# Seven products in the second and third feed-forward layers, input sums made over four tiles, and the modulation stream moved into the down projections

## The chip, the cores and the metric

The kernel runs on one core of one Trainium2 chip. The metric is device time in microseconds (us), the median over several runs. The engines are named as the profile names them: PE (TensorE, matrix products), PEld (its weight loads), DVE (VectorE), ACT (ScalarE), POOL (GpSimd) and SP (SyncE, which here issues the DMA transfers). Each engine works through its own queue of instructions in order.

## The reference

Two encoder layers, each of a feed-forward network (FFN), a mixer and a second FFN, on x of 512 tokens by 1024 channels, float32. The mixer is a state-space layer (SSM) in the first layer, an attention in the second. The core of it:

```python
def modulate(x, m): return x * (1 + m[:, 1][:, None, :]) + m[:, 0][:, None, :]
def swiglu(u, w_gate, w_up, w_down):
    return (jax.nn.silu(u @ w_gate) * (u @ w_up)) @ w_down
cond = jax.nn.silu(c)
for i in range(DEPTH):                                   # DEPTH = 2
    mods = (cond @ ada_w[i] + ada_b[i]).reshape(b, N_SUB, 3, D_MODEL)
    gate = lambda s: (1 + mods[:, s, 2])[:, None, :]
    y = swiglu(modulate(x, mods[:, 0]), ffn_w_gate[i, 0], ffn_w_up[i, 0], ffn_w_down[i, 0])
    x = layer_norm(ALPHA * x + 0.5 * gate(0) * y, ln_g[i, 0], ln_b[i, 0])
    u = modulate(x, mods[:, 1])
    y = mamba2_bidir(...) if i % 2 == 0 else diff_attention(...)
    x = layer_norm(ALPHA * x + gate(1) * y, ln_g[i, 1], ln_b[i, 1])
    y = swiglu(modulate(x, mods[:, 2]), ffn_w_gate[i, 1], ffn_w_up[i, 1], ffn_w_down[i, 1])
    x = layer_norm(ALPHA * x + 0.5 * gate(2) * y, ln_g[i, 2], ln_b[i, 2])
```

The FFN's inner width is 2816 = 22 x 128. `mods` is the product of the vector `cond` with a 1024 x 9216 matrix in each layer.

## The kernel before

Activations lie transposed: 8 arrays of 128 channels by 512 tokens. A float32 product is made of three products in a shorter format: every operand is split into a high part (`hi`, `uh`, `wh`: a copy by ACT) and the rest (`lo`, `ul`, `wl`: a subtraction on DVE), and `mm3` (L162) multiplies hi by hi, hi by lo and lo by hi.

The six parts of the program are numbered n = 0 to 5: FFN, SSM, FFN, FFN, attention, FFN. Below they are FFN0, FFN2, FFN3 and FFN5. An FFN has 22 tiles (f0 to f21), each of 128 columns of the inner width, cut into three parts of 8, 7 and 7 tiles. A part makes its tiles (gate and up products, `h = silu(gate) * up` at L538, and the split of h) and then its share of the down projection: 8 units of 128 output channels, each added to the residual stream `resid` by `add_res` (L366). In the last part of each FFN the layer norm (`LN`) is worked in, half the tokens at a time.

There are two ways to make a tile:

- The standard tile: 48 products of 512 columns: 8 input blocks, 3 products each, for gate and for up. Its two weight arrays (`wgu`, 128 x 1024 each) are loaded to `raw`, and `split` makes `wh` on ACT (L119) and `wl` on DVE (L120).
- The tile of seven products (`seven`): with the input cut in halves of the inner dimension and of the tokens, the two-by-two block product is made of 7 products instead of 8, as in Strassen's method: 7 x 4 blocks x 3 = 84 products of 256 columns. It needs sums of the weights (`weight_forms`: four additions on DVE in place, L461, and four splits, L451 and L452) for each tile, sums of products (L484 to L500), and sums of the inputs once per FFN (`input_forms`, L427 to L432).

`input_forms` makes four sets, one for each pair of input blocks k and k + 4. A set is 2 additions of 128 x 512 (`ft`, `fb`), 4 additions or subtractions of 128 x 256, and two splits. Before the change only FFN5 uses the seven products, from tile f4 on (`first7=4`), and all four sets are written at its tile f1.

The adaLN modulation `mods` is a stream of 144 loads of 512 KB (`adaw`), each followed by one multiply-and-sum on DVE over 128 x 1024 (`ada_unit`, L180). `advance(stream, k)` takes the next k of them. 16 are made at the start; FFN0 takes 3 per tile, FFN2 and FFN3 take 2 per tile after tile f3; these 72 belong to the second layer.

All loads of weights and of the stream go through one ring of 4 buffers (`raw`), issued by SP in program order (L93); the split weights have 3 + 3 buffers; temporary arrays (`tmp`) 6. At the start of FFN2, FFN3 and FFN5, POOL rescales the residual stream, 16 instructions (L359, L360 in `residual`). The scheduler of the framework, not the program text alone, sets the order of the instructions in each engine's queue; waits between engines follow from the data.

## Time and profile before

| | |
|---|---|
| median of 3 runs | 2255.68 us (2252.91 to 2257.87) |
| the profiled execution's own time | 2252.16 us |
| its span, first to last instruction | 2250.4 us |
| mean granted TensorE clock | 0.992 of full speed |
| PE busy | 2190.8 us, 97% |
| DVE busy | 1477.0 us, 66% |
| ACT busy | 900.0 us, 40% |
| POOL busy | 408.1 us, 18% |
| DMA, mean | 132 GB/s |

A busy share is an average over stages with different limits; the stages are read one by one in the rows below. Idle time of an engine costs nothing unless others wait for what it does next. "Releaser" names what ended an engine's wait, by the profile.

### The profile page before, as it was taken

The page shows a single profiled execution, that of the slowest core. Times are in us where ns is not written, and L with a number is a line of the kernel's source. Part 1 is how long each engine was busy: PE and PEld are TensorE (multiplying, and loading weights), DVE is VectorE, ACT ScalarE, POOL GpSimd, SP SyncE. Part 2 cuts the span into 40 slices and gives each one's busy share as a digit, 9 for nine tenths or more (in the row PEclk, how much of TensorE's full clock was granted, in tenths as well). Part 3 has the DMA queues.
Part 4 walks back from the last instruction along what each step waited for, and adds up shares of the span by engine and source line. Part 5 has one row for each costly group of instructions (what it writes and reads, how often), then busy time and mean ns, then how long its engine had stood idle before and what let it go on. Part 6 is the DMA issues. An engine that isn't in the chain of part 4 may idle for free.

```text
span 2250.4 us, 30448 instructions
## 1 busy us (share of the span) xinstructions
PE 2190.8 (97%) x11734; PEld 1825.4 (81%) x11734; DVE 1477.0 (66%) x2358; ACT 900.0 (40%) x1480; POOL 408.1 (18%) x412
## 2 busy tenths in 40 slices
PE   7999999999999989999999999999999999899998
PEld 5788888866777778888889888888877779889897
DVE  6865557656675788354558544545866679959696
ACT  4422223567656543222233222223555544525353
POOL 2000003344322336000015200003300025000003
PEclk9999999999999999999999999999999999999999
DMA  8865552465544416354642545542211121323231
GB/s 300 284 207 168 188 189 77 113 183 141 161 122 130 127 57 216 123 178 130 196 122 84 188 151 160 157 132 84 67 57 57 57 64 50 113 85 106 92 114 46
DMA packets 88529, 296.75 MB, mean 132 GB/s; under 512 B 9536, under 2 KB 12992, under 8 KB 88384
## 3 DMA queue, kind: packets, MB, share of 16 engines
q1 hardware_dynamic: 88384, 294.81, 42.2%
q8 instruction: 92, 1.51, 0.3%
q14 instruction: 53, 0.43, 0.1%
HBM read 289.53 MB, written 5.24 MB: 131 GB/s over the span
## 4 chain that ended last, share of the span: by engine, by line
PE 68%; DVE 7%; issue 4%; POOL 2%; ACT 1%; DMA 0%; POOLq 0%; ACTq 0%; DVEq 0%
PE acc L162 58%; PE mid L162 3%; PE mid L781 1%; DVE ul L350 1%; DVE wl L120 1%; PE mid L930 1%; PE ln L162 1%; DVE lt L348 1%; PE ln L249 1%; POOL E L770 1%; PE ln L729 1%; DVE lo L150 0%; DVE sc L292 0%; DVE resid L321 0%; ACT wh L119 0%
## 5 line engine op out<-in xcount | busy, mean ns | idle before, releaser
L119 ACT ACTIVATE wh<-raw 128x1024 fp32r<-128x1024 f32 (+1 forms) x306 | 316.0, 1035 | 752.9 <-PE acc L162 479.7
L162 PE MATMUL acc<-uh,wl 128*128 128x512 f32 (+1 forms) x1544 | 583.9, 378 | 7.4 <-DVE wl L120 7.4
L162 PE MATMUL acc<-uh,wh 128*128 128x512 f32 (+1 forms) x1544 | 587.3, 381 | 0.0
L162 PE MATMUL acc<-ul,wh 128*128 128x512 f32 (+1 forms) x1544 | 585.0, 379 | 0.4 <-DVE ul L1038 0.4
L120 DVE TENSOR_TENSOR wl<-raw,wh 128x1024 fp32r<-128x1024 f32 (+1 forms) x306 | 374.1, 1224 | 151.7 <-ACT wh L119 140.1
L162 PE MATMUL acc<-hi,wh 128*128 128x512 f32 (+1 forms) x1200 | 424.1, 354 | 6.1 <-DVE resid L366 6.1
L162 PE MATMUL acc<-hi,wl 128*128 128x512 f32 (+1 forms) x1200 | 423.7, 353 | 0.0
L162 PE MATMUL acc<-lo,wh 128*128 128x512 f32 (+1 forms) x1200 | 423.2, 353 | 0.0
L162 PEld LDWEIGHTS acc<-uh,wl 128*128 128x128 f32 x1544 | 291.8, 189 | 66.2 <-DVE wl L120 8.7
L162 PEld LDWEIGHTS acc<-uh,wh 128*128 128x128 f32 x1544 | 291.6, 189 | 63.4 <-issue 9.4
L162 PEld LDWEIGHTS acc<-ul,wh 128*128 128x128 f32 x1544 | 292.1, 189 | 58.4 <-issue 4.7
L180 DVE SCALAR_TENSOR_TENSOR raw<-raw,cond 128x1024 f32<-128x1024 f32 x144 | 178.1, 1241 | 160.9 <-DMA raw<-in_adaw 160.3
L162 PEld LDWEIGHTS acc<-hi,wh 128*128 128x128 f32 x1200 | 228.6, 191 | 40.6 <-DVE resid L366 6.5
L162 PEld LDWEIGHTS acc<-hi,wl 128*128 128x128 f32 x1200 | 229.0, 191 | 31.0 <-issue 1.2
L162 PEld LDWEIGHTS acc<-lo,wh 128*128 128x128 f32 x1200 | 228.9, 191 | 31.0 <-issue 0.8
L366 DVE SCALAR_TENSOR_TENSOR resid<-acc,gv,resid 128x512 f32<-128x512 f32 (+1 forms) x172 | 113.4, 661 | 123.9 <-PE acc L162 123.4
L112 POOL TENSOR_TENSOR wal<-raw,wah 128x512 fp32r<-128x512 f32 x13 | 21.4, 1649 | 879.1 <-ACT wah L110 879.1
L538 DVE TENSOR_TENSOR h<-sg,acc 128x512 f32<-128x512 f32 x65 | 44.5, 686 | 115.1 <-PE acc L162 114.8
L451 ACT ACTIVATE wh<-raw 128x1024 fp32r<-128x1024 f32 x54 | 57.1, 1059 | 85.5 <-PE acc L162 58.1
L162 PE MATMUL acc<-uh,wah 128*128 128x256 f32 (+1 forms) x232 | 65.4, 304 | 13.4 <-ACT wah L110 11.5
L277 POOL TENSOR_TENSOR resid<-resid,m 128x512 f32<-128x512 f32 x12 | 20.6, 1737 | 293.6 <-ACT m L274 292.0
L359 POOL TENSOR_TENSOR resid<-resid,rs 128x512 f32<-128x512 f32 x40 | 65.3, 1653 | 39.0 <-ACT rs L353 39.0
(270 smaller groups left out, 3189.3 us busy)
## 6 DMA issues: line engine op xcount, KB each, us to landing
raw<-in_wgu SPq DMA_DIRECT2D x176, 512.0 KB, 4.2
raw<-in_adaw SPq DMA_DIRECT2D x144, 512.0 KB, 4.4
raw<-in_wdn SPq DMA_DIRECT2D x64, 448.0 KB, 3.4
raw<-in_win SPq DMA_DIRECT2D x40, 512.0 KB, 4.0
raw<-in_wdn SPq DMA_DIRECT2D x32, 512.0 KB, 4.4
rw<-scr SPq DMA_DIRECT2D x32, 512.0 KB, 5.6
ch<-scr SPq DMA_DIRECT2D x32, 256.0 KB, 3.6
raw<-in_wso SPq DMA_DIRECT2D x16, 512.0 KB, 3.7
```

The costliest lines, as they stand in the source:

```text
L119: nc.scalar.activation(hi[:, :n], raw, AF.Copy)
L120: nc.vector.tensor_tensor(out=lo[:, :n], in0=raw, in1=hi[:, :n].bitcast(F32), op=ALU.subtract)
L162: last = nc.tensor.matmul(o, lhsT=a, rhs=b, start=start and j == 0, stop=j == n - 1, skip_group_check=not start)
L180: nc.vector.scalar_tensor_tensor(out=raw, in0=raw, scalar=1.0, in1=cond, op0=ALU.mult, op1=ALU.mult, accum_out=mods[l][:, j : j + 1],)
L249: nc.tensor.matmul(o[:, j * P : (j + 1) * P], lhsT=cols[:, j : j + 1].broadcast_to([P, P]), rhs=ident, start=True, stop=True)
L348: nc.vector.scalar_tensor_tensor(out=t, in0=res[d][:, a:b], scalar=G, in1=rb, op0=ALU.mult, op1=ALU.mult)
L350: nc.vector.scalar_tensor_tensor(out=ul, in0=t, scalar=B, in1=uh.bitcast(F32), op0=ALU.add, op1=ALU.subtract)
L359: nc.gpsimd.tensor_tensor(out=res[d], in0=res[d], in1=self.rs, op=ALU.mult)
L366: nc.vector.scalar_tensor_tensor(out=res[d][:, a:b], in0=pd[:, a:b], scalar=gvec[n][:, d : d + 1], in1=res[d][:, a:b], op0=ALU.mult, op1=A ...
L451: nc.scalar.activation(x[0], r, AF.Copy)
L538: nc.vector.tensor_tensor(out=h, in0=sg, in1=pu, op=ALU.mult)
L729: nc.tensor.matmul(pst, lhsT=bt[:, i * P : (i + 1) * P], rhs=xd, start=o == 0, stop=o == 1)
```

## The change

It calls FFN2 and FFN3 with `first7=4` too, so their tiles f4 to f21 become tiles of seven products. The four sets of input sums are no longer written at tile f1, but one at a time behind `h` of the four tiles before `first7`: f0 to f3 in FFN2, FFN3 and FFN5. The condition no longer asks whether the FFN has tiles of seven products at all. FFN0 keeps the default `first7=22`, and so writes four sets at its tiles f18 to f21 that nothing reads. The stream takes two numbers: per standard tile, and per down unit of the first two parts. FFN0 stays at 3 per tile. FFN2 and FFN3 take 1 per standard tile (4 of them) and 2 per down unit (16 units), 36 each, and none in their tiles of seven.

```diff
     def input_forms(u):
-        forms = []
         for k in range(4):
             top, bot = tmp("ft"), tmp("fb")
...
-            forms.append({
+            yield {
                 1: half(u[k], 0), 2: half(u[k + 4], 0), 3: half(u[k + 4], 1),
                 5: half((th, tl), 0), 7: half((th, tl), 1), 4: half((bh, bl), 0), 6: half((bh, bl), 1),
-            })
-        return forms
+            }
...
-    def ffn(n, stream=None, per=0, pre=None, first7=FT):
+    def ffn(n, stream=None, per=(0, 0), pre=None, first7=FT):
+        forms, making = [], None
...
             for _ in range(nf):
-                if f == 1 and first7 < FT:
-                    forms = input_forms(u)
                 if f >= first7:
...
                     f += 1
-                    advance(stream, per)
                     continue
...
                 hs.append(split_act(h))
+                if first7 - 4 <= f < first7:
+                    making = making or input_forms(u)
+                    forms.append(next(making))
                 f += 1
-                if f > 3:
-                    advance(stream, per)
+                if f > 3 or n > 0:
+                    advance(stream, per[0])
...
             for _ in down_units(n, hs, [mk(d) for d in range(KT)], pi == len(FPARTS) - 1):
-                pass
+                if pi < 2:
+                    advance(stream, per[1])
...
-    ffn(0, st0, 3, [[k[j] for k in ks] for j in range(8)])
+    ffn(0, st0, (3, 0), [[k[j] for k in ks] for j in range(8)])
...
-    ffn(2, st1, 2)
-    ffn(3, st1, 2)
+    ffn(2, st1, (1, 2), first7=4)
+    ffn(3, st1, (1, 2), first7=4)
```

How it moves instructions is seen in the queues' order. On DVE in FFN2, before the change, the stretch from tile f3's `h` holds splits of weights (L120), splits of `h` (L150) and products of the stream (L180):

```order
L538 TENSOR_TENSOR h_7649<-sg_7647,acc_7622 128x512
L120 TENSOR_TENSOR wl_7822<-raw_7819,wh_7821 128x1024
L150 TENSOR_TENSOR lo_7652<-h_7649,hi_7651 128x512
L180 SCALAR_TENSOR_TENSOR raw_7959,mods1_87<-raw_7959,cond_73 128x1024
L180 SCALAR_TENSOR_TENSOR raw_7962,mods1_87<-raw_7962,cond_73 128x1024
L120 TENSOR_TENSOR wl_7892<-raw_7889,wh_7891 128x1024
```

After the change, around tile f2's and f3's `h` (L535 now), the same queue holds the third set of input sums (L426 to L431), and the weight sums (L459) and splits (L450) of the first tile of seven, f4, whose raw weights are `raw_7795` and `raw_7797`; `wl_7908` and `w4l_7914` are the next tile's:

```order
L429 TENSOR_TENSOR ft_7687<-ft_7687,fb_7688 128x256
L459 TENSOR_TENSOR raw_7797<-raw_7797,raw_7795 128x512
L430 TENSOR_TENSOR fb_7688<-fb_7688,ft_7687 128x256
L150 TENSOR_TENSOR lo_7696<-ft_7687,hi_7695 128x512
L431 TENSOR_TENSOR fb_7688<-fb_7688 128x256
L459 TENSOR_TENSOR raw_7795<-raw_7797,raw_7795 128x512
L450 TENSOR_TENSOR wl_7802<-raw_7797,wh_7801 128x1024
L150 TENSOR_TENSOR lo_7700<-fb_7688,hi_7699 128x512
L459 TENSOR_TENSOR raw_7795<-raw_7795 128x512
L450 TENSOR_TENSOR wl_7908<-raw_7903,wh_7907 128x1024
L450 TENSOR_TENSOR w4l_7914<-raw_7905,w4h_7913 128x512
L450 TENSOR_TENSOR wl_7804<-raw_7795,wh_7803 128x1024
```

The last row, `wl_7804`, is the third weight form of f4, and the set's sums and another tile's splits now stand ahead of it. On PE after the change, the first product of f4 (into `acc_7819`) needs only the direct weights; the second (into `acc_7820`) starts at the 13th product of f4 and needs the third form, `wh_7803` and `wl_7804`:

```order
L162 MATMUL acc_7819<-uh_7160,wh_7799 128x256
L162 MATMUL acc_7819<-ul_7161,wh_7799 128x256
L162 MATMUL acc_7819<-uh_7160,wl_7800 128x256
L162 MATMUL acc_7820<-hi_7431,wh_7803 128x256
L162 MATMUL acc_7820<-lo_7432,wh_7803 128x256
L162 MATMUL acc_7820<-hi_7431,wl_7804 128x256
```

So between the first and the second group of products PE now depends on that DVE row. The products that read the fourth set of input sums stand further back in PE's queue: the last array that DVE makes of that set is first read at the 75th product counted from f4's first. On SP, in the first down projection of FFN2, the 8 loads of down weights stood in a row before (`in_wdn 128x1024 x8`). Now two loads of the stream follow each of them:

```order
L93 DMA raw_8303<-in_wdn0 128x1024
L93 DMA raw_8335<-in_adaw 128x1024
L93 DMA raw_8338<-in_adaw 128x1024
L93 DMA raw_8341<-in_wdn0 128x1024
L93 DMA raw_8373<-in_adaw 128x1024
L93 DMA raw_8376<-in_adaw 128x1024
```

The two stream loads wait for a free `raw` buffer, and the next load of down weights is queued behind them.

## Rows read from the trace of the kernel before

**Rows 1.** The page: busy time of each engine with its share of the span and its instructions; and the chain that ended last, its shares of the span by engine.

```profile
PE 2190.8 (97%) x11734; PEld 1825.4 (81%) x11734; DVE 1477.0 (66%) x2358; ACT 900.0 (40%) x1480; POOL 408.1 (18%) x412
PE 68%; DVE 7%; issue 4%; POOL 2%; ACT 1%; DMA 0%; POOLq 0%; ACTq 0%; DVEq 0%
```

**Rows 2.** Busy time of each engine by stretch (us; in brackets the number of instructions), then the granted clock, the DMA share and GB/s. In order: tiles with the stream in FFN0; three of its last tiles before the last down projection; the start of FFN2 while POOL rescales; five standard tiles of FFN2; a down projection of FFN2; the start of FFN5 while POOL rescales; three us behind a pause in FFN5; six tiles of seven in FFN5.

```profile
69.00:104.00 35.00, 35.00 (x153) 28.61 (x153) 29.36 (x46) 14.10 (x16) 0.00 (x0) 1.00 0.87 293
313.30:345.10 31.80, 31.80 (x140) 26.02 (x139) 10.43 (x14) 8.39 (x12) 0.00 (x0) 1.00 0.41 129
851.00:888.00 37.00, 37.00 (x250) 34.26 (x250) 32.17 (x37) 13.89 (x18) 36.57 (x16) 1.00 0.75 247
989.60:1044.70 55.10, 55.10 (x241) 45.07 (x240) 23.96 (x32) 15.46 (x21) 0.00 (x0) 1.00 0.48 150
1054.40:1088.20 33.80, 33.80 (x148) 27.65 (x147) 20.56 (x27) 7.26 (x8) 0.00 (x0) 1.00 0.59 184
1888.50:1916.70 28.20, 26.97 (x198) 25.16 (x197) 28.20 (x32) 8.69 (x12) 28.13 (x16) 1.00 0.22 76
1923.00:1926.00 3.00, 2.96 (x7) 2.39 (x8) 2.96 (x5) 0.00 (x0) 0.00 (x0) 0.50 0.56 175
2022.30:2082.10 59.80, 59.80 (x501) 59.50 (x500) 54.83 (x84) 29.89 (x47) 0.00 (x0) 1.00 0.34 101
```

**Rows 3.** The timeline of DVE: start, duration, engine, line. The last addition of each part's down projection, three for FFN2, three for FFN3, three for FFN5.

```profile
973.00 0.75 DVE L366 SCALAR_TENSOR_TENSOR resid<-acc,gv,resid 128x512 f32<-128x512 f32 x1
1088.19 0.75 DVE L366 SCALAR_TENSOR_TENSOR resid<-acc,gv,resid 128x512 f32<-128x512 f32 x1 [1.62 <-PE acc L162]
1207.63 0.47 DVE L366 SCALAR_TENSOR_TENSOR resid<-acc,gv,resid 128x256 f32<-128x256 f32 x1
1343.54 0.75 DVE L366 SCALAR_TENSOR_TENSOR resid<-acc,gv,resid 128x512 f32<-128x512 f32 x1 [0.46 <-PE acc L162]
1459.35 0.75 DVE L366 SCALAR_TENSOR_TENSOR resid<-acc,gv,resid 128x512 f32<-128x512 f32 x1 [1.59 <-PE acc L162]
1578.68 0.47 DVE L366 SCALAR_TENSOR_TENSOR resid<-acc,gv,resid 128x256 f32<-128x256 f32 x1
2015.77 0.75 DVE L366 SCALAR_TENSOR_TENSOR resid<-acc,gv,resid 128x512 f32<-128x512 f32 x1 [3.52 <-PE acc L162]
2124.98 0.75 DVE L366 SCALAR_TENSOR_TENSOR resid<-acc,gv,resid 128x512 f32<-128x512 f32 x1 [2.63 <-PE acc L162]
2237.64 0.49 DVE L366 SCALAR_TENSOR_TENSOR resid<-acc,gv,resid 128x256 f32<-128x256 f32 x1
```

**Rows 4.** The timeline of PE in FFN5: the end of one run of products, the pause in square brackets with its releaser, the first product back at the shorter duration, and the first product of 256 columns of f4.

```profile
1915.90 0.39 PE L162 MATMUL acc<-ul,wh 128*128 128x512 f32 x1
1923.04 0.79 PE L162 MATMUL acc<-uh,wl 128*128 128x512 f32 x1 [6.75 <-DVE wl L120]
...
1928.25 0.39 PE L162 MATMUL acc<-uh,wl 128*128 128x512 f32 x1
...
1930.57 0.28 PE L162 MATMUL acc<-uh,wh 128*128 128x256 f32 x1
```

**Rows 5.** The timeline of DVE at the start of FFN5: f0's `h`, some of the input sums that follow, and what stands between the last of them and f3's weights. A next start minus a start is the time that an instruction took of the queue.

```profile
1895.29 0.68 DVE L538 TENSOR_TENSOR h<-sg,acc 128x512 f32<-128x512 f32 x1
...
1896.49 1.78 DVE L427 TENSOR_TENSOR fb<-uh,ul 128x512 f32<-128x512 f32 x1
...
1909.30 1.10 DVE L150 TENSOR_TENSOR lo<-ft,hi 128x512 fp32r<-128x512 f32 x1
...
1918.70 0.41 DVE L431 TENSOR_TENSOR fb<-fb,ft 128x256 f32<-128x256 f32 x1
1919.03 0.68 DVE L150 TENSOR_TENSOR lo<-ft,hi 128x512 fp32r<-128x512 f32 x1
...
1921.77 1.22 DVE L120 TENSOR_TENSOR wl<-raw,wh 128x1024 fp32r<-128x1024 f32 x1
...
1923.50 1.22 DVE L452 TENSOR_TENSOR wl<-raw,wh 128x1024 fp32r<-128x1024 f32 x1
1924.64 0.68 DVE L150 TENSOR_TENSOR lo<-h,hi 128x512 fp32r<-128x512 f32 x1
1925.24 0.68 DVE L452 TENSOR_TENSOR w4l<-raw,w4h 128x512 fp32r<-128x512 f32 x1
```

**Rows 6.** The timelines of DVE (f0's `h` in FFN2 and FFN3) and of PE (the first 512-column product of f3 in FFN2, FFN3 and FFN5).

```profile
854.90 0.69 DVE L538 TENSOR_TENSOR h<-sg,acc 128x512 f32<-128x512 f32 x1
1225.48 0.69 DVE L538 TENSOR_TENSOR h<-sg,acc 128x512 f32<-128x512 f32 x1 [0.15 <-ACT sg L536]
872.66 0.40 PE L162 MATMUL acc<-uh,wh 128*128 128x512 f32 x1
1243.83 0.39 PE L162 MATMUL acc<-uh,wh 128*128 128x512 f32 x1
1910.19 0.40 PE L162 MATMUL acc<-uh,wh 128*128 128x512 f32 x1
```

**Rows 7.** The timeline of SP: seven loads of down weights, 512 KB each, in FFN0; one product of the stream on DVE in FFN2; and the waits of DVE in 850 to 1210 for such loads (us in total, times, longest).

```profile
92.29 11.16 SPq L93 DMA_DIRECT2D raw<-in_wdn  x7
868.36 1.21 DVE L180 SCALAR_TENSOR_TENSOR raw<-raw,cond 128x1024 f32<-128x1024 f32 x1
DVE raw L180 <- DMA raw<-in_adaw: 57.9, 29, 5.2
```

## The prediction, made before the changed kernel ran

> **What bounds the kernel now.** I read the page first: PE is busy in 97% of the span, and the chain that ended last lies on PE for 68% of it [rows 1]. So the kernel pays for PE work, and for the few places where PE stands still. The reader is to see in the stretches that this holds in the FFNs: five standard tiles took 55.10 us with PE busy throughout, 11.02 us each, DVE only 23.96 us of it; in FFN5 six tiles of seven took 59.80 us with PE busy throughout, 9.97 us each, but DVE was busy 54.83 us of it, 92% [rows 2]. A tile of seven thus gives PE 1.05 us less work and leaves DVE 8% of slack. More DVE work in such a tile hides only up to 0.8 us.
>
> Next I read PE's timeline at FFN5's start, where the only tiles of seven begin. PE stops after 1915.90 for 6.75 us, ended by DVE's split of f3's weights [rows 4]. That split (1921.77) stood in DVE's queue behind all four sets of input sums [rows 5]. Behind the pause the granted clock is 0.50, the 1.2 GHz level [rows 2], until 1928.25 [rows 4]. f3's first 512-column product stood at 1910.19 [rows 6]; a tile later would be 1921.2; f4's first product came at 1930.57 [rows 4]. The burst of sums costs FFN5 9.3 us in all.
>
> **What is saved on PE.** The part periods show it without any arithmetic on products. From the last addition of part 1 to that of part 2: 115.19 us in FFN2, 115.81 in FFN3, 109.21 in FFN5; from part 2 to part 3: 119.44, 119.33 and 112.66 [rows 3]. Where FFN2 and FFN3 become like FFN5, they gain 6.0 + 6.6 and 6.8 + 6.7, together 26.1 us. In part 1 four of the eight tiles change, 4 x 1.05 = 4.2 us per layer, 8.4 in both. Saving: **34.5 us**.
>
> **What the sums cost at f4.** Prices on DVE, start to start: 0.60 us for 128x512, 0.33 for 128x256, 1.14 for 128x1024 [rows 5]; a product of the stream 1.14 as well (1.21 with its drain [rows 7]). One set of sums is four of the first kind and four of the second, 3.7 us. PE's second group of products in f4 needs the third weight form of f4. Counting DVE's queue of the changed kernel from f0's `h` to that row: FFN2 24, 12, 8 of the three kinds and 2 of the stream, 29.8 us; FFN3 23, 12, 6 and 1 and four tiny ones, 26.3 us; FFN5 23, 12, 5, 23.5 us.
>
> To this comes what POOL takes. While its 16 rescaling instructions run (28.13 us in FFN5, 36.57 in FFN2 [rows 2]), some DVE instructions stretch: a 128x512 sum at 1896.49 lasts 1.78 us, against 0.68 undisturbed [rows 5]. The 17 instructions from 1895.29 to 1909.30 (10 of 0.60, 7 of 0.33, 8.3 us) took 14.0 us, 5.7 us more; carried to POOL's end at 1916.7 that is 8.7 us. The bounds are 0 and 8.7. I take 8 for FFN5, where it is seen, and 7 for FFN2 and FFN3, nearer to the upper end, because there too DVE now has sums of two SBUF inputs under nearly all of POOL's time.
>
> PE would reach the row's first reader, the 15th product of f4, at f3's first product + 11.05 + 14 x 0.119: from f0's `h`, 30.5 us in FFN2 (872.66 - 854.90 = 17.8), 31.1 in FFN3 (1243.83 - 1225.48 = 18.4), 27.6 in FFN5 (1910.19 - 1895.29 = 14.9) [rows 6, 5]. So PE waits
> - in FFN2 36.8 - 30.5 = 6.3 us. Behind the 6.75 us pause 5.2 us passed at the lower level (1923.04 to 1928.25), which cost half of it, 2.6; I take 2.5 here. Two products of the stream (2.3 us) now stand ahead of f0's `h` too and may make it late; I take 1 of it. Together 9.8;
> - in FFN3 33.3 - 31.1 = 2.2 us. I put the clock at 1.7. The fourth set of sums, due about 8.8 us into f4 (74 products), comes at 44.6 against 42.1: 2.5 and again 1.7 for the clock: 8.1;
> - in FFN5 31.5 - 27.6 = 3.9 and 1.7, and the fourth set 2.4 and 1.7: 9.7, where the burst cost 9.3: +0.4.
> After a pause of 2 us the clock may not fall at all; without its cost the three terms are 9 us smaller together (2.5, 3.4 and 3.4). With POOL's stretching at its bounds the pauses are all but gone at 0, and 4 us longer in sum at 8.7.
>
> **The stream in the down projections.** DVE is busy 20.56 of 33.80 us there [rows 2], about 2.96 us in a unit of 4.87 us. Two products of the stream add 2.3, so the unit is over DVE's time by some 0.4 at worst, but the tiles of seven ahead have their preparation done early: over a part of 7, the count of DVE's queue at the same prices gives 97 to 98.5 us of work for the 109.2 that FFN5's part took [rows 3]. Loads: 8 of down weights, 16 of the stream and 4 for the next tiles share 4 buffers. A down load took 11.16 / 7, 1.6 us, in FFN0 under load [rows 7], and 293 GB/s with 87% DMA share is 1.79 us for 512 KB [rows 2]. At 1.7 us, 28 loads take 48 us; a part of 7 has 39 us of down units and, by the tiles' preparation running ahead, an estimated 16 more: covered, with up to 7 us in hand. Before, DVE waited 57.9 us for stream loads in 29 waits and PE did not notice [rows 7, 2]. I charge 0.5 us to each of four down phases, **+2**. The tiles of FFN2 and FFN3 lose two loads and 2.3 us of DVE work each, which is what makes room for the weight sums.
>
> **The dead sums in FFN0.** Four sets, 15 us of DVE over four tiles. DVE is busy there 10.43 of 31.80 us [rows 2]; 3.7 more per 11 us tile is covered by the idle two thirds: 0. If `h` were late by a whole set once, 3.7; I keep 1 as the bound.
>
> **Sum.** -34.5 + 9.8 + 8.1 + 0.4 + 2 = -14.2 us. The profiled execution took 2252.16 (2250.4 span and 1.8 around it), 0.16% under the median; on the median of 2255.68 that is **2241 us**.
>
> **Rivals.**
> 1. *The spread hides the sums.* One set per tile, 3.7 us, beside 11.05 us tiles, and no stop at f4; FFN5's 9.3 us then go too. For it: outside POOL's stretch DVE in standard tiles has over half of its time free [rows 2]. Against: without POOL the count of DVE's queue stays only 0.7, 4.8 and 4.1 us under PE's time, so it holds only if POOL stretches less than seen before. -34.5 - 9.3, plus 2 to 12 for small waits: 2214 to 2224. Chance 0.18.
> 2. *POOL and DVE shut each other out.* The Trainium skill, page "SBUF — State Buffer", section "Who interferes with whom", states that a VectorE instruction with two inputs in SBUF and a GpSimd instruction that reads SBUF exclude each other for a whole instruction. As a mechanism here: with POOL's 28 us added whole to DVE's queue [rows 2], the pauses are 29.8 + 28 - 30.5 = 27 in FFN2, 23 in FFN3 and 24 in FFN5, less the 9.3 of before: -34.5 + 27 + 23 + 24 - 9.3 + 2 = +32, 2288. The row speaks against the full price: DVE did 8.3 us of work in 14.0 us under POOL [rows 5], a loss of 0.4 of the time, so part overlaps. The trace agrees with the rule's direction and not with its full price. Chance 0.04.
> 3. *The stream chokes the down projections* (the other side). If a load takes t us, a part of 7 needs 28 t in 55 us. From t = 1.96 on, each 0.1 us costs 2.8 us in each of the four phases, so the gain of 14.2 is gone at t = 2.09; 2.2 gives 4 x 6.7 - 14.2 = +13, 2268. The rate that 1.6 to 1.8 us show [rows 2, 7] speaks against; that each buffer now comes free only after ACT or DVE has read it speaks for it. Chance 0.08.
> 4. *The pauses eat the gain*: at one and a half times to twice what I charge in FFN2 and FFN3, because more than one row of f4 comes late, 9 to 18 us more: 2250 to 2259. DVE's order with another tile's splits ahead of f4's third form speaks for it, the 92% that hold in FFN5 without a pause [rows 2] against. Chance 0.12.
>
> The forecast, with its own range of 2230 to 2249, holds 0.58. Leaving out about a tenth at either end (half of rival 1, and rivals 2 and 3 with the end of 4) gives 2217 to 2258. The 0.2% that a measurement of this kernel can tell is 4.5 us: faster 0.79 (the forecast, rival 1 and the lower end of 4), same 0.09, slower 0.12.
>
> **What would show it.** Tiles of seven in FFN2 and FFN3 at 9.97 us, periods of 109 and 112.7 between the last additions. A pause of PE within f4 of FFN2, FFN3 and FFN5, ended by DVE's split of a weight sum or of an input sum, with the clock at 0.50 behind it. No pause for DMA in the down projections, a unit still 4.87 us. FFN0's span unchanged. It is wrong if PE shows no stop at f4 (rival 1), if the stops pass 10 us under POOL's instructions (rival 2), or if PE waits in the down projections for splits whose load was late (rival 3).

## The result, and the profile after

The changed kernel took 2259.88 us (median of 18 runs, 2256.72 to 2263.75) against 2254.80 us for the kernel before on the same chips: ratio 1.0023, interval 1.0017 to 1.0030. It is 5 us (0.2%) slower. 2241 us was predicted, with faster as the likeliest sign.

The page after, busy time by engine and the chain by engine, as [rows 1]:

```profile
PE 2170.5 (96%) x13030; PEld 1866.5 (83%) x13030; DVE 1746.3 (77%) x2850; ACT 989.0 (44%) x1648; POOL 403.5 (18%) x412
PE 54%; DVE 17%; issue 5%; ACT 3%; DMA 2%; POOL 2%; POOLq 0%; ACTq 0%; DVEq 0%; SPq 0%
```

PE is busy 20.3 us less, DVE 269 us more. PE's share of the chain that ended last fell from 68% to 54%, and DVE's rose from 7% to 17%. PE's work did get less, but it now waits: the time between its instructions rose by some 29 us. It also ran longer at a granted clock of 0.50, where half of PE's busy time is lost: 20.2 us in this trace and 13.0 before. With that taken out PE's busy time fell by 27.5 us.

The last additions of the nine parts, in DVE's timeline, as [rows 3]:

```profile
983.43 0.74 DVE L366 SCALAR_TENSOR_TENSOR resid<-acc,gv,resid 128x512 f32<-128x512 f32 x1
1097.25 0.75 DVE L366 SCALAR_TENSOR_TENSOR resid<-acc,gv,resid 128x512 f32<-128x512 f32 x1
1216.86 0.47 DVE L366 SCALAR_TENSOR_TENSOR resid<-acc,gv,resid 128x256 f32<-128x256 f32 x1
1361.15 0.75 DVE L366 SCALAR_TENSOR_TENSOR resid<-acc,gv,resid 128x512 f32<-128x512 f32 x1 [1.81 <-PE acc L162]
1474.64 0.74 DVE L366 SCALAR_TENSOR_TENSOR resid<-acc,gv,resid 128x512 f32<-128x512 f32 x1
1586.67 0.47 DVE L366 SCALAR_TENSOR_TENSOR resid<-acc,gv,resid 128x256 f32<-128x256 f32 x1
2023.84 0.75 DVE L366 SCALAR_TENSOR_TENSOR resid<-acc,gv,resid 128x512 f32<-128x512 f32 x1 [3.52 <-PE acc L162]
2133.10 0.75 DVE L366 SCALAR_TENSOR_TENSOR resid<-acc,gv,resid 128x512 f32<-128x512 f32 x1 [2.63 <-PE acc L162]
2245.76 0.48 DVE L366 SCALAR_TENSOR_TENSOR resid<-acc,gv,resid 128x256 f32<-128x256 f32 x1
```

Their differences say where the time went. The first column of each FFN runs from the last addition of the stage ahead (834.68 before, 834.21 after in FFN2; 1871.32 and 1879.44 in FFN5). The other kernels of this study are in the same table, so that each can be read by stage (one profiled execution each, us):

| kernel | FFN2 part 1 | part 2 | part 3 | FFN3 part 1 | part 2 | part 3 | FFN5 part 1 |
|---|---|---|---|---|---|---|---|
| before | 138.32 | 115.19 | 119.44 | 135.91 | 115.81 | 119.34 | 144.46 |
| after | 149.22 | 113.82 | 119.61 | 144.29 | 113.49 | 112.03 | 144.40 |
| e1_guard | 148.99 | 113.01 | 118.76 | 144.28 | 112.55 | 112.63 | 145.56 |
| e2_std_none | 148.02 | 113.78 | 112.02 | 143.42 | 114.00 | 112.23 | 145.52 |
| e3_six | 140.76 | 112.53 | 120.27 | 138.62 | 109.18 | 113.14 | 137.45 |
| e4_act_resid | 155.60 | 113.97 | 118.59 | 141.89 | 112.55 | 112.06 | 143.42 |
| e5_resid_late | 143.15 | 112.37 | 119.08 | 138.22 | 112.53 | 111.58 | 142.62 |
| e6_down_late | 149.86 | 111.77 | 112.04 | 144.55 | 111.74 | 111.61 | 144.42 |
| e7_burst | 159.49 | 113.03 | 119.47 | 144.52 | 114.82 | 113.00 | 145.65 |
| e8_six_late | 138.16 | 110.88 | 112.35 | 137.50 | 110.30 | 111.63 | 137.47 |
| e9_five_late | 142.36 | 111.35 | 112.24 | 137.69 | 110.56 | 111.62 | 139.57 |
| e10_four_resid | 145.97 | 111.84 | 112.03 | 142.04 | 111.01 | 111.62 | 139.30 |
| e11_tile_stream | 150.31 | 109.66 | 121.79 | 147.23 | 109.20 | 114.10 | 144.44 |
| e12_no_seven | 144.45 | 117.69 | 125.46 | 137.52 | 117.04 | 119.35 | 144.40 |

Before to after: +10.9, -1.4, +0.2, +8.4, -2.3, -7.3 and -0.1 us, +8.4 in all; the two profiled executions differ by 8.8 us, the medians by 5.1. One execution of a stage is not exact: FFN3's part 2 lies between 112.53 and 114.82 us in the five kernels that leave the stream and the tiles of seven as the change has them (after, e1, e4, e5, e7). Only one stage of six, FFN3's part 3, has the whole gain of its tiles (7.3 us). Three places took it back in the others.

**The first tiles of seven.** PE's timeline at f4 of FFN2, and at f4 of FFN3; then the stretches around these pauses, with columns as in [rows 2]:

```profile
893.47 0.58 PE L162 MATMUL acc<-hi,wh 128*128 128x256 f32 x1 [6.53 <-ACT wh L449]
895.25 0.58 PE L162 MATMUL acc<-hi,wl 128*128 128x256 f32 x1 [0.99 <-DVE wl L450]
```

```profile
1267.33 0.38 PE L162 MATMUL acc<-hi,wh 128*128 128x256 f32 x1 [1.60 <-ACT wh L449]
1270.12 0.39 PE L162 MATMUL acc<-hi,wl 128*128 128x256 f32 x1 [2.29 <-DVE wl L450]
1276.17 0.58 PE L162 MATMUL acc<-uh,wh 128*128 128x256 f32 x1 [2.87 <-ACT px L482]
```

```profile
893.40:899.00 5.60, 4.55 (x20) 4.25 (x21) 5.60 (x11) 1.01 (x4) 0.00 (x0) 0.51 0.37 132
1270.00:1282.00 12.00, 9.01 (x46) 8.72 (x47) 11.53 (x19) 5.39 (x8) 0.00 (x0) 0.57 0.40 131
```

In FFN2 the 7.5 us of pause stand at the second group of products, as forecast, with DVE busy throughout and the granted clock near 0.5 behind the pause. In FFN3 3.9 of the 6.8 us stand there. The third pause, 2.87 us, is another: PE waits to write an accumulator that ACT reads late (`px`, L482), because that reading stands in ACT's queue behind weight copies (L449) which wait for DVE's weight sums. The lower clock costs 2.2 us in FFN2 and 3.7 in FFN3: it lasts from 892.0 to 898.8 and from 1270.9 to 1281.1, PE is busy for 4.35 and 7.4 us of that, and half of this time is lost.

**FFN2's layer norm.** DVE's timeline in the last down projection of FFN2, which the change gives no stream load; the wait of PE that follows; and the stretch behind it:

```profile
1191.91 2.31 DVE L180 SCALAR_TENSOR_TENSOR raw<-raw,cond 128x1024 f32<-128x1024 f32 x1
1194.14 0.08 DVE L180 DVE_READ_ACCUMULATOR raw<-raw,cond 128x1 f32 x1
1194.14 1.13 DVE L366 SCALAR_TENSOR_TENSOR resid<-acc,gv,resid 128x512 f32<-128x512 f32 x2
...
1197.78 1.75 DVE L180 SCALAR_TENSOR_TENSOR raw<-raw,cond 128x1024 f32<-128x1024 f32 x1
1199.47 0.08 DVE L180 DVE_READ_ACCUMULATOR raw<-raw,cond 128x1 f32 x1
1199.47 0.47 DVE L366 SCALAR_TENSOR_TENSOR resid<-acc,gv,resid 128x256 f32<-128x256 f32 x1
```

```profile
1202.61 0.75 PE L299 MATMUL mid<-sc,onesd 128*128 128x256 f32 x1 [3.66 <-DVE sc L292]
```

```profile
1203.00:1208.00 5.00, 5.00 (x23) 4.82 (x23) 3.13 (x13) 0.33 (x1) 0.71 (x1) 0.50 0.01 3
```

These products of the stream belong to FFN3's first standard tiles. Three of the four loads were issued ahead, and the scheduler set their products in DVE's queue among the last residual additions of FFN2, where the layer norm waits for each addition. The products did not wait for their loads here. They simply took DVE's time, and beside POOL's sums of the layer norm they took 1.65, 2.31 and 1.75 us, against 1.21 undisturbed [rows 7].

**The end of part 2.** The timelines of SP, DVE, ACT and PE in FFN2, the last tiles of part 2, in one chain:

```profile
1028.62 7.18 SPq L93 DMA_DIRECT2D raw<-in_adaw  x2
```

```profile
1034.21 1.23 DVE L180 SCALAR_TENSOR_TENSOR raw<-raw,cond 128x1024 f32<-128x1024 f32 x1 [2.26 <-DMA raw<-in_adaw]
1035.36 0.08 DVE L180 DVE_READ_ACCUMULATOR raw<-raw,cond 128x1 f32 x1
1035.36 0.69 DVE L459 TENSOR_TENSOR raw<-raw 128x512 f32<-128x512 f32 x1
```

```profile
1037.01 1.06 ACT L449 ACTIVATE wh<-raw 128x1024 fp32r<-128x1024 f32 x1 [4.66 <-DVE raw L459]
```

```profile
1040.64 0.39 PE L162 MATMUL acc<-hi,w4h 128*128 128x256 f32 x1 [1.56 <-ACT sg L488]
```

DVE stands 2.26 us for a stream load with the weight sums (L459) of the last tile behind it; ACT waits 4.66 us for such a sum; PE waits for ACT, which reads the accumulator (`sg`, L488) only behind its weight copies. The next pause of PE stands behind a late load too, but on ACT:

```profile
1051.04 0.95 ACT L119 ACTIVATE wh<-raw 128x896 fp32r<-128x896 f32 x1 [2.46 <-DMA raw<-in_wdn]
1051.90 0.36 ACT L488 ACTIVATE sg<-acc 128x256 f32<-128x256 f32 x1
```

```profile
1052.32 0.39 PE L162 MATMUL acc<-hi,w4h 128*128 128x256 f32 x1 [1.41 <-ACT sg L488]
```

ACT's copy of down weights (L119) waits for a load that SP issued behind two stream loads, and the reading that PE needs stands behind that copy. The same copy waits 2.75 us ahead of FFN2's pause of 0.95 us at 1063.13, and 3.00 us ahead of the longest one in FFN3's part 2 (1.45 at 1440.14). Before the change ACT's waits show none for a down load in these two parts. Part 2 so has 4.4 us of pauses in FFN2 and 2.2 in FFN3, where it had none before.

### The profile page after: what moved, and what is told of

Its sections match the earlier page's. It is cut to its first block, busy times and chain, and to the rows that moved or that the text cites. A ratio compares the mean times of both kernels' runs of the same rounds, so it can differ in the third digit from the quotient of the medians.

```text
span 2259.2 us, 33641 instructions
## 1 busy us (share of the span) xinstructions
PE 2170.5 (96%) x13030; PEld 1866.5 (83%) x13030; DVE 1746.3 (77%) x2850; ACT 989.0 (44%) x1648; POOL 403.5 (18%) x412
## 4 chain that ended last, share of the span: by engine, by line
PE 54%; DVE 17%; issue 5%; ACT 3%; DMA 2%; POOL 2%; POOLq 0%; ACTq 0%; DVEq 0%; SPq 0%
PE acc L162 42%; PE mid L162 5%; DVE wl L120 2%; DVE raw L459 2%; PE mid L782 2%; DVE lo L150 1%; DVE wl L450 1%; DMA raw<-in_wdn 1%; DVE ul L350 1%; DVE raw L180 1%; PE mid L931 1%; PE ln L162 1%; DVE lt L348 1%; ACT wh L119 1%; PE ln L249 1%
## 5 line engine op out<-in xcount | busy, mean ns | idle before, releaser
L162 PE MATMUL acc<-hi,wh 128*128 128x512 f32 (+1 forms) x1488 | 506.6, 341 | 20.0 <-ACT wh L449 10.0
L162 PE MATMUL acc<-uh,wh 128*128 128x512 f32 (+1 forms) x1256 | 442.6, 353 | 4.5 <-ACT px L482 4.4
L162 PE MATMUL acc<-ul,wh 128*128 128x512 f32 (+1 forms) x1256 | 439.7, 350 | 0.1
L162 PE MATMUL acc<-uh,wl 128*128 128x512 f32 (+1 forms) x1256 | 438.5, 350 | 1.3 <-DVE wl L120 1.3
L119 ACT ACTIVATE wh<-raw 128x1024 fp32r<-128x1024 f32 (+1 forms) x234 | 239.2, 1027 | 410.1 <-PE acc L162 212.1
L120 DVE TENSOR_TENSOR wl<-raw,wh 128x1024 fp32r<-128x1024 f32 (+1 forms) x234 | 288.0, 1232 | 86.5 <-ACT wh L119 77.5
L449 ACT ACTIVATE wh<-raw 128x1024 fp32r<-128x1024 f32 x162 | 170.8, 1059 | 211.1 <-DVE raw L459 107.6
L180 DVE SCALAR_TENSOR_TENSOR raw<-raw,cond 128x1024 f32<-128x1024 f32 x144 | 179.5, 1254 | 52.4 <-DMA raw<-in_adaw 52.0
L450 DVE TENSOR_TENSOR wl<-raw,wh 128x1024 fp32r<-128x1024 f32 x162 | 197.0, 1220 | 28.6 <-ACT wh L449 27.7
L459 DVE TENSOR_TENSOR raw<-raw 128x512 f32<-128x512 f32 x216 | 150.3, 698 | 4.4
L162 PE MATMUL mid<-uh,wh 128*128 128x256 f32 (+2 forms) x332 | 94.8, 286 | 1.0 <-DVE up L491 0.9
L162 PE MATMUL mid<-uh,wl 128*128 128x256 f32 (+2 forms) x332 | 94.0, 284 | 0.6 <-DVE wl L120 0.6
```

What stands on the lines that cost most here:

```text
L119: nc.scalar.activation(hi[:, :n], raw, AF.Copy)
L120: nc.vector.tensor_tensor(out=lo[:, :n], in0=raw, in1=hi[:, :n].bitcast(F32), op=ALU.subtract)
L162: last = nc.tensor.matmul(o, lhsT=a, rhs=b, start=start and j == 0, stop=j == n - 1, skip_group_check=not start)
L180: nc.vector.scalar_tensor_tensor(out=raw, in0=raw, scalar=1.0, in1=cond, op0=ALU.mult, op1=ALU.mult, accum_out=mods[l][:, j : j + 1],)
L449: nc.scalar.activation(x[0], r, AF.Copy)
L450: nc.vector.tensor_tensor(out=x[1], in0=r, in1=x[0].bitcast(F32), op=ALU.subtract)
```

## The experiments

All started from the changed kernel. Times are medians, ratios are to the kernel before on the same chip (2253.55 us beside e1 to e4, 2252.32 beside e5 to e8, 2253.70 beside e9 to e12). Runs of different groups are best compared by their ratios; the changed kernel has 1.0023.

**e1_guard: no dead sums in FFN0.**

```diff
-                if first7 - 4 <= f < first7:
+                if first7 < FT and first7 - 4 <= f < first7:
```

> The changed kernel, but FFN0 makes no input sums (the condition asks again whether the FFN has tiles of seven). If the dead sums are hidden: the same time as the changed kernel, ratio to before 1.002 to 1.003, FFN0's parts unchanged (118.3 and 116.8 us between last additions). If they cost: 3 us or more less, with FFN0's last part shorter by that.

2260.08 us, ratio 1.0028 (1.0012 to 1.0045): the changed kernel's time within its interval. The dead sums are hidden.

**e2_std_none: no stream loads on standard tiles of FFN2 and FFN3.**

```diff
-            for _ in down_units(...):
+            for d, _ in enumerate(down_units(...)):
                 if pi < 2:
-                    advance(stream, per[1])
+                    advance(stream, per[1] + (n > 0 and pi == 0 and d % 2))
...
-    ffn(2, st1, (1, 2), first7=4)
-    ffn(3, st1, (1, 2), first7=4)
+    ffn(2, st1, (0, 2), first7=4)
+    ffn(3, st1, (0, 2), first7=4)
```

> The changed kernel, but FFN2 and FFN3 take no stream load on their standard tiles; the four of each go to every second unit of the first down projection (3 there in place of 2). If the loads of FFN3's first tiles cost the pause in FFN2's layer norm: FFN2's part 3 falls from 119.6 to about 112.7 us, the pause of 3.66 us there and its slow clock go, and each of the pauses at the start of FFN2 and FFN3 shrinks by 1 to 3 us: 9 to 13 us less than the changed kernel, about 2248. If the layer norm waits for POOL's sums instead: FFN2's part 3 stays at 119 and only 2 to 4 us go.

2252.34 us, 0.9992 (0.9982 to 1.0002). FFN2's part 3 fell from 119.61 to 112.02 us, the pause in the layer norm is gone. That part of the first reading holds. The starts of FFN2 and FFN3 gained only 1.2 and 0.9 us, at the low end, and the total of 7 us by the ratios fell short of the 9 to 13 expected.

**e3_six: tiles of seven from f6 on**, in FFN2, FFN3 and FFN5, sums at f2 to f5 (`first7=6` in the three calls).

> The changed kernel with the tiles of seven from f6 on in FFN2, FFN3 and FFN5, the four sets of sums at f2 to f5. Six tiles stay standard: 6 x 1.05 = 6.3 us more PE work. If the pauses at the first tile of seven come from DVE being late in the stretch where POOL works and the sums are made: two tiles more (22 us) let DVE catch up, the pauses of FFN2, FFN3 (15 and 12.6 us with the clock) and FFN5 (9) go for the most part: 20 to 30 us less than the changed kernel, about 2230 to 2240. If DVE is simply full and the pause only moves to f6: 0 to 6 us more than the changed kernel.

2237.98 us, 0.9930 (0.9915 to 0.9945). The three part 1 lost 8.5, 5.7 and 7.0 us in spite of 2.1 us more PE work in each. So DVE is not full for good: it is behind at the start only, and the pause doesn't move on in full. The pause in FFN2's layer norm stayed (120.27). FFN3's part 2 is 109.18, the full gain, with the stream's loads where the changed kernel has them: their place alone does not make the loss there.

**e4_act_resid: half of the rescaling on ACT.**

```diff
-                    nc.gpsimd.tensor_scalar(
-                        out=res[d], in0=res[d], scalar1=lnag[n][:, d : d + 1],
-                        scalar2=lnab[n][:, d : d + 1], op0=ALU.mult, op1=ALU.add,
-                    )
+                    nc.scalar.activation(
+                        res[d], res[d], AF.Identity, bias=lnab[n][:, d : d + 1], scale=lnag[n][:, d : d + 1]
+                    )
```

> The changed kernel with the second half of the residual's rescaling (8 instructions per layer norm, 1.98 us each on POOL) made by ACT. POOL's stretch at the start of FFN2, FFN3 and FFN5 falls from some 30 to about 12 us. If POOL's instructions stretch DVE's and so set the pauses: DVE's stretched instructions are half as many, each of the three pauses falls by 4 to 5 us and its clock loss with it, 12 to 20 us less than the changed kernel. If DVE's own work sets them: within 3 us of the changed kernel.

2269.19 us, 1.0067 (1.0052 to 1.0082): slower, which neither theory had. ACT's timeline in FFN2 and PE's wait show why:

```profile
856.62 0.82 ACT L360 ACTIVATE resid<-resid,lnab,lnag 128x512 f32<-128x512 f32 x1 [1.42 <-POOL resid L359]
858.85 0.81 ACT L360 ACTIVATE resid<-resid,lnab,lnag 128x512 f32<-128x512 f32 x1 [1.41 <-POOL resid L359]
...
868.63 1.05 ACT L119 ACTIVATE wh<-raw 128x1024 fp32r<-128x1024 f32 x1
```

```profile
869.73 0.58 PE L162 MATMUL mid<-uh,wh 128*128 128x256 f32 x1 [7.43 <-ACT wh L119]
```

ACT stood in its own queue for POOL, eight times, with the weight copies behind it. FFN3's and FFN5's part 1 got 2.4 and 1.0 us shorter. The run says nothing clean on POOL, because it moved the wait to ACT.

**e5_resid_late: the rescaling waits for f5.** DVE's queue has the same instructions in the same order as in the changed kernel.

```diff
-            ln.residual()
+            late_res[0] = ln.residual
+            if n in (0, 3):
+                ln.residual()
...
+                    if after is not None:
+                        tc.add_manual_dep(x.ins, after.ins.name, SYNC, reason="later")
...
+                    if f == 6:
+                        late_res[0](last_sg[0])
```

> The changed kernel, but POOL's 16 rescaling instructions at the start of FFN2, FFN3 and FFN5 wait for the product sums of tile f5, so they run behind the pause instead of under the input sums; DVE's queue keeps its order. If POOL's instructions stretch DVE's (about 8 us in each of the three stretches): the stretched steps of 1.5 to 2.3 us vanish from DVE's rows ahead of f4, the pauses there (7.5, 6.8 and 5.6 us, and 4 to 5 us of slow clock each) go nearly all, and the kernel takes 15 to 30 us less than the changed one, less what the same instructions cost in f6 and f7 (up to 5 us each). If DVE's own work sets the pauses: within 3 us of the changed kernel.

2242.36 us, 0.9952 (0.9938 to 0.9967), 16 us less than the changed kernel by the ratios. POOL's and DVE's timelines in FFN2 of the changed kernel: a rescaling pair, f0's `h`, the first stretched steps, and the third weight form of f4:

```profile
863.24 4.75 POOL L360 TENSOR_SCALAR resid<-resid,lnag,lnab 128x512 f32<-128x512 f32 x2
```

```profile
856.64 0.68 DVE L535 TENSOR_TENSOR h<-sg,acc 128x512 f32<-128x512 f32 x1
...
859.80 2.31 DVE L120 TENSOR_TENSOR wl<-raw,wh 128x1024 fp32r<-128x1024 f32 x1
862.03 1.50 DVE L429 TENSOR_TENSOR ft<-ft,fb 128x256 f32<-128x256 f32 x1
...
893.98 1.22 DVE L450 TENSOR_TENSOR wl<-raw,wh 128x1024 fp32r<-128x1024 f32 x1
```

The same four in DVE's timeline of this run, where POOL's first rescaling starts at 908.68:

```profile
853.27 0.67 DVE L543 TENSOR_TENSOR h<-sg,acc 128x512 f32<-128x512 f32 x1
...
856.01 1.21 DVE L120 TENSOR_TENSOR wl<-raw,wh 128x1024 fp32r<-128x1024 f32 x1
857.15 0.41 DVE L435 TENSOR_TENSOR ft<-ft,fb 128x256 f32<-128x256 f32 x1
...
881.99 1.21 DVE L456 TENSOR_TENSOR wl<-raw,wh 128x1024 fp32r<-128x1024 f32 x1
```

From `h` to the weight form: 37.34 us with POOL beside it, 28.72 without, for the same queue, with no idle time of DVE between in either. POOL cost DVE 8.6 us. Measured alike it is 9.1 us in FFN3 and 8.3 in FFN5. PE has no pause at f4 of FFN2 any more; part 1 fell by 6.1, 6.1 and 1.8 us. It fell by less than the pauses because POOL now runs beside the first tiles of seven, with pauses of 0.7 to 1.8 us there; in FFN5 a granted clock of 0.50 from 1865.6 to 1872.4, ahead of its first tile, costs 3.4 us besides. POOL's instructions are shown to be the cause of most of the pauses at f4.

**e6_down_late: e2, and the stream from the third down unit on, three loads a unit.**

```diff
+            for d, _ in enumerate(down_units(...)):
-                if pi < 2:
+                if pi < 2 and n > 0 and d > 1:
                     advance(stream, per[1])
...
+    ffn(2, st1, (0, 3), first7=4)
+    ffn(3, st1, (0, 3), first7=4)
```

> As the run without stream loads on standard tiles, but in the down projections of the first two parts the stream starts only at the third unit, three loads a unit (18 a part, 36 a layer). If a product of the stream that waits for its load in DVE's queue ahead of the last tile's weight sums makes the pauses near the end of part 2: part 2 of FFN2 and FFN3 falls from 113.8 and 114.0 to 109.2 to 110, some 8 us less, about 2244. If those pauses come from DVE being full or from the raw buffers as such: part 2 stays at 113 to 114 and the time at 2252.

2249.80 us, 0.9988 (0.9979 to 0.9998): 1 us under e2 by the ratios, where 8 was expected, and the intervals overlap. Part 2 fell by 2.0 and 2.3 us to 111.8 and 111.7, not to 109.2, and part 1 rose by 1.8 and 1.1. Products of the stream still wait in DVE's queue, now ahead of the result sums of the last tiles, and ACT's copies of down weights still wait for their loads (5.05 us for one in FFN3). So this run does not settle the cause; e11 does more.

**e7_burst: all four sets of sums behind f0.**

```diff
-                if first7 - 4 <= f < first7:
-                    making = making or input_forms(u)
-                    forms.append(next(making))
+                if f == 0 and first7 < FT:
+                    forms.extend(input_forms(u))
```

> The changed kernel with all four sets of input sums behind f0, as FFN5 had them before. If what counts is the amount of DVE's work ahead of f4 and not its place: within 4 us of the changed kernel, with FFN5's part 1 at 144.4 either way. If the spread is what keeps DVE ahead: each of the three starts 4 us or more longer, 12 us or more in all.

2272.58 us, 1.0090 (1.0075 to 1.0105), 15 us more than the changed kernel by the ratios, most of it in FFN2's part 1 (159.49): one pause there is 18.04 us, for f2's weights behind the sums. FFN3's and FFN5's part 1 differ by 0.2 and 1.3 us. So the spread matters in FFN2 and hardly in the other two; neither theory had this.

**e8_six_late: e3, e6 and e1 together.** `first7=6` and `(0, 3)`, with the stream from the third unit on and the guard.

> Tiles of seven from f6 on, no stream on standard tiles, the stream in the down projections from the third unit on, no dead sums in FFN0. If the three causes are separate and add: the 22 us that f6 gave, the 7 us of FFN2's layer norm and 3 us of FFN2's part 2 are all had: 2225 to 2231, about 1.2 percent under the kernel before. If they overlap (a pause removed at one place comes back at another): 2234 to 2240, no better than f6 alone.

2223.57 us, 0.9873 (0.9858 to 0.9888): 1.3% faster than the kernel before, the best of all here, and just under the 2225 to 2231 of the first reading. The gains add, and a little more: every part 1 is at 137.5 to 138.2, part 3 at 111.6 to 112.4. Only part 2 is still 1 to 1.7 us over FFN5's 109.2.

**e9_five_late: the same from f5 on** (`first7=5`).

> As the run with tiles of seven from f6 and the late stream in the down projections, but from f5 on, sums at f1 to f4. Three tiles more of seven save 3 x 1.05 = 3.2 us. If one tile's time (11 us) past f4 is enough for DVE to catch up behind POOL: 2219 to 2222. If part of the pause comes back (DVE's delay of 8 us from POOL against the 11 us gained leaves 1 to 3 us in each FFN, with the clock): 2223 to 2230.

2230.63 us, 0.9896 (0.9881 to 0.9911), just above the second reading. It is slower than from f6, though the intervals overlap a little. FFN2's part 1 is 4.2 us longer than in e8, with pauses of 1.1 and 1.5 us soon after the first tile of seven begins; FFN5's is 2.1 longer. By these traces one tile is not enough room.

**e10_four_resid: e5, e6 and e1 together.**

> Tiles of seven from f4 on, with all other cures: POOL's rescaling behind f5, no stream on standard tiles, the stream in the down projections from the third unit on, no dead sums in FFN0. If the gains add: the 17 us of the late rescaling and the 10 us of the stream's two moves, 2230 to 2236. If POOL's instructions, now under tiles of seven where DVE has 8 percent of slack, are what is left: pauses of 1 to 3 us in f5 to f8 of each FFN. No pause at f4.

2238.04 us, 0.9934 (0.9919 to 0.9948), above the 2230 to 2236 of added gains. No pause over 1 us at f4, but pauses of up to 2.9 us later in part 1 of FFN2 and FFN3, beside POOL's rescaling (911 to 944 us in FFN2). The second reading holds for the most part: POOL's work costs there too, where DVE is near full.

**e11_tile_stream: the stream back on the tiles, two loads each from f3 on.**

```diff
                     f += 1
+                    advance(stream, per[0])
                     continue
...
-                if f > 3 or n > 0:
+                if f > 3:
                     advance(stream, per[0])
...
+    ffn(2, st1, (2, 0), first7=4)
+    ffn(3, st1, (2, 0), first7=4)
```

> The changed kernel with the stream put back to two loads on each tile from f3 on, tiles of seven too, none in the down projections. DVE then has 9.14 us of a tile of seven and 2.29 of the stream, 11.4 us against PE's 9.97. If DVE becomes the bound: 1.5 us on each of some 30 tiles, less the pauses of the down projections and of FFN2's layer norm (16 us): 2280 to 2300. If the stream's products hide in the waits of DVE: 2240 to 2250.

2260.03 us, 1.0034 (1.0020 to 1.0047): the same as the changed kernel, far from either expectation. Part 2 is 109.66 and 109.20, the full gain; the pauses near its end are gone. So what the stream's loads and products do in the down projections made them. What it saves there it gives back in part 1 (+1.1, +2.9) and part 3 (+2.2, +2.1). The stretch 1000 to 1060 in FFN2, tiles of seven with the stream:

```profile
1000.00:1060.00 60.00, 59.78 (x476) 57.77 (x475) 57.55 (x96) 28.38 (x43) 0.00 (x0) 1.00 0.55 175
```

DVE is busy 57.55 of 60 us and PE doesn't wait. The products of the stream (8 in this stretch) fit, because weights prepared ahead carry the stretch: it makes six tiles, but holds the weight sums of four (16 rows of L459). Over the whole part DVE is busy 97.0 of 109.66 us. DVE's slack counts over a part, not over a tile.

**e12_no_seven: the stream's new place and FFN5's spread alone**, FFN2 and FFN3 with standard tiles and no sums, and the guard of e1.

```diff
-                if f > 3 or n > 0:
+                if (f > 3) == (n == 0) or f == 4:
...
+    ffn(2, st1, (1, 2))
+    ffn(3, st1, (1, 2))
```

> The changed kernel without its tiles of seven in FFN2 and FFN3, and without the dead sums: the stream's new places (one load on each of f0 to f3, two on a down unit of the first two parts) and the spread sums in FFN5 alone. If the pause in FFN2's layer norm belongs to the stream's loads for FFN3's first tiles: FFN2's part 3 is 5 to 8 us longer than before (119.4), FFN2's and FFN3's part 2 within 1 us of before, since standard tiles leave DVE idle; 2257 to 2262. If it belongs to the tiles of seven: the kernel before, 2252 to 2255.

2268.19 us, 1.0063 (1.0040 to 1.0086): 14.5 us over the kernel before, more than expected (interval 9 to 19). FFN2's part 3 is 6.0 us longer, so the pause in the layer norm doesn't need the tiles of seven. But part 1 and part 2 of FFN2 are 6.1 and 2.5 us longer too, FFN3's 1.6 and 1.2. In FFN2's part 1, DVE's and PE's timelines:

```profile
932.28 1.23 DVE L180 SCALAR_TENSOR_TENSOR raw<-raw,cond 128x1024 f32<-128x1024 f32 x1 [2.46 <-DMA raw<-in_adaw]
...
935.55 0.68 DVE L535 TENSOR_TENSOR h<-sg,acc 128x512 f32<-128x512 f32 x1
```

```profile
936.95 0.80 PE L162 MATMUL acc<-hi,wh 128*128 128x512 f32 x1 [2.78 <-ACT hi L149]
```

The last tile's `h` stood behind products of the stream that waited for their loads, and the down projection's products need its split. In the changed kernel PE's pause at that place is only 0.61 us (942.08). By this run the move of the stream costs 14.5 us with no tile of seven in FFN2 and FFN3; the spread in FFN5 adds nothing to it (144.46 before, 144.40 here).

## Why the prediction was wrong

**The saving of 34.5 us** was right for parts 2 and 3 (26.1 of it), where a run shows them without pauses: FFN3's part 3 gained 7.3 (6.7 said); in e11 part 2 gained 5.5 and 6.6 (6.0 and 6.6 said); in e2 FFN2's part 3 gained 7.4 (6.8 said). The 8.4 us of part 1 no run shows by itself: with the lower clock taken out, PE's busy time there fell by 1.1 us in FFN2 and 2.6 in FFN3, where 4.2 was said for each.

**The starts, 9.8 and 8.1 us, were under-sized.** Part 1 rose by 10.9 and 8.4 us where 4.2 us less work was to come: 15.1 and 12.6. The mechanism, the place of the first pause and DVE's own work held: 28.72 us were measured without POOL from `h` to the start of the row, where the count gives 29.8 to its end, 1.14 later. Mis-sized was POOL's stretching (7 taken; 8.6 and 9.1 measured). The pauses at f4 are 7.5 us in FFN2 (7.3 said) and 6.8 in FFN3 (4.7 said), the clock cost 2.2 and 3.7 us (2.5 and 3.4 said), and FFN2's part 1 has four more pauses of 0.5 to 0.7 us ahead of f4 and behind the last tile. FFN3's charge of 2.5 us for the fourth set of sums was wrong in kind: no pause stands there, and the third pause is ACT's late reading. The rest of the 15.1 and 12.6, some 3.1 and 1.6 us, is neither pause nor clock but work in part 1 that did not get less; why stays open. The bound of 8.7 us of POOL was taken as an upper end, and FFN3 lies above it.

**FFN5's +0.4** was near: -0.1. Its pauses at f4 are 6.3 us (6.3 said), 1.5 of them again for ACT's late reading, and its clock cost 2.0 (3.4 said).

**The stream, +2 us, is the step that failed.** It cost 8.9 us in the two part 2 (gains of 1.4 and 2.3 in place of 6.0 and 6.6) and 7.0 us in FFN2's part 3, 15.9 in all. The pauses and the clock that the trace shows in these three parts come to 14.5 us of it. The loads were priced for SP and for the buffers, and DVE's queue was given a sum over the part. Both came out near (22 loads from 1040.44 to 1076.91, 1.7 us each; DVE busy 100.7 of 113.8 us in FFN2's part 2), and neither was the point. What decided was the order in the queues. A product of the stream stood in DVE's queue ahead of work that PE needed next, in part 2 with its load not yet there; a copy of down weights stood so in ACT's queue, with its load issued behind the stream's. One sentence of the prediction led away from that: that PE did not notice DVE's 57.9 us of waits for stream loads before [rows 7]. They stood in stretches where DVE had half its time free [rows 2]. And the layer norm had no term at all, since the change gives its part no load; three of the four loads of FFN3's standard tiles were issued ahead into it. The loss in part 2 is shown to come with the stream in the down projections (e11), and the one in the layer norm with the loads of the tiles (e2). How the part 2 loss divides between DVE's queue and ACT's, and why e3 has none in FFN3, stays open.

The sum by measured terms: -34.5 + 15.1 + 12.6 - 0.1 + 8.9 + 7.0 - 0.6 (FFN3's part 3 over its term) = +8.4. The terms are differences from the table, so this only shows that none is left out.

**FFN0's dead sums at 0** were right (e1).

**DVE's 8% of slack**, which was said to hide only 0.8 us per tile, was wrong as a rule for each tile: e11 put 8 products of the stream in six tiles' time with no pause, with the weight sums of two of the tiles made ahead.

**The rivals.** The first (spread hides the sums) fell: PE stops at f4. The second, a full exclusion of POOL and DVE, fell on its price (8.3 to 9.1 us per start, not 28), but its mechanism is there and larger than the forecast had it. The Trainium skill, page "SBUF — State Buffer", section "Who interferes with whom", names the pair that e5 shows to clash, a VectorE instruction with two inputs in SBUF and a GpSimd one that reads SBUF. The trace agrees as to the pair: every stretched row has two inputs in SBUF, and the seven rows of `h` beside POOL, which read one of theirs from an accumulator, kept 0.67 to 0.69 us. That the whole of POOL's time is lost to DVE no run here shows. The third (the stream chokes the down projections) named the right part of the change, and its sign came: PE waits at the end of part 2 behind copies whose load was late. But the rate of loads, by which it was priced, held at 1.7 us; the order of the queues did it. The fourth came nearest to the time, 2250 to 2259, by one and a half to twice the charge at f4. Part 1 did lose 1.5 times the charge, though pauses and clock alone were 1.2 and 1.4 times of it, and the stream did the rest: its time was right in part by luck.

What stays open: why e7's burst hurts FFN2 so much more than FFN3 and FFN5, and which part of the clock loss at each start (2.2 and 3.7 us) follows from the first pause and which from the next ones.

## What to carry to other kernels

A product that waits for a load, or only takes time, holds up everything behind it in its engine's queue: before moving such work, list what stands behind each of these rows and who waits for it, also in the stages that get none by the program text, and on the other engines whose loads now come behind the moved ones. Work for a new phase (here the input sums and the first tiles of seven) is best begun where nothing else slows its engine: moving the start by two tiles cost 6.3 us of PE work and returned some 27. Cures of separate waits added up here: by the ratios 21 us for the start, and 13 more for the stream's moves, to 1.3% under the kernel before.

## What the runs showed of the hardware

With POOL's 16 rescaling instructions beside it, the same DVE queue took 37.34 us in place of 28.72 in FFN2; a 128x256 step lasted 1.50 us in place of 0.41, a 128x1024 one 2.31 in place of 1.21. Not every step is stretched. A stretched one took about 0.4 or 1.1 us more, whatever its size, and all of them have two inputs in SBUF. The loss is about a third of the time that POOL is busy in the same stretch (8.6 of 27.7 us in FFN2, 9.1 of 23.1 in FFN3, 8.3 of 23.2 in FFN5).

In FFN3 PE stood 1.60 and 2.29 us, with half a microsecond of work between, and the granted clock then fell to 0.50, the 1.2 GHz level; over the 12 us from 1270, with a third pause of 2.87 us in them, it was 0.57. In FFN2's part 2 pauses of 1.56 and 1.41 us, 12 us apart, left it at 1.00.
